# A decoder layer on one core: the input norm without GpSimd, regrouped S5 transfers, ScalarE-issued Toeplitz loads, earlier row maxima

## The chip, the cores and the metric

The kernel runs on one core of a Trainium2 chip. The metric is the device time of one execution in microseconds; three runs of the kernel before gave 2133.14, 2130.14 and 2130.84 us, median 2130.84. All inputs and outputs are float32 in HBM. Each float32 matrix product is carried out as three products of rounded parts ("high" and "low" tiles in the type fp32r: high x high, high x low, low x high), so nearly every operand has to be split on ScalarE (high copy) and VectorE (difference) before TensorE can read it.

## The reference

One layer over 1024 tokens of width 1024:

```python
h = rmsnorm(x, norm_mix)
proj = h @ w_in                      # 3 x 512 FoX, 8 log-forget, 512 S5, 4 x 512 HGRN, 3 x 1024 gates
q, k = rmsnorm(fq), rmsnorm(fk)      # per head, 8 heads x 64
y_fox = softmax(q k^T / 8 + c_i - c_j, causal) @ v      # c = cumsum(log_sigmoid(ff + bias))
y_s5 = glu(gelu(diagonal_state_space(su)))   # 32 groups x 16 channels, 64 complex states each
y_hg = rmsnorm(hgrn2(hq, hf, hi)) * silu(hg) # 4 heads, 128 x 128 state, chunks of 64
gates = sigmoid(gl)
x = x + (gates[0]*(y_fox @ wb0) + gates[1]*(y_s5 @ wb1) + gates[2]*(y_hg @ wb2)) @ w_out
x = x + cross_attention(rmsnorm(x), rmsnorm(mem))       # 4 heads, 256 memory rows
x = x + (silu(a) * b) @ w_down, where a, b = rmsnorm(x) @ w_gate_up
```

## The kernel before, in words

Activations lie with channels on the 128 partitions and tokens along the free dimension; weight tiles are the stationary operand. Every product goes through `proj`, a generator that yields after a few matmuls of 512 columns. On-chip memory is an arena of 50 equal slots (`u(name)` takes the next free one), and PSUM is handed out by bank (`psm`). A scheduler orders the instructions of each engine by a running priority; `ahead(n, fn)` emits what `fn` does as if it stood n places earlier. All DMAs before the change are issued from SP's queue, which runs them in order.

The stages run in this order: input norm and the first projections `su`, the S5 mixer, the forgetting attention (`fox_main`), the HGRN mixer (`hg_main`), then gate 0 with the branch projection of the attention, the S5 glu, gate 1, gate 2, output projection, cross attention and feed-forward. The mixers are chains of small steps on several engines, so projections of later stages are put between them as filler: `drive` runs one step of the mixer and then `pump` emits filler for a planned number of us of TensorE. In the S5 stage a step is followed by `S5_US` (4.5 us) times a weight from `S5_W`: the entries stand for preparation, its second part, the body and the output (`s5_prep`, `s5_prep2`, `s5_body`, `s5_out`, which belong to blocks o, o-1, o-2 and o-3 of a round; the round runs preparation, output, second part, body). Work given to `later(us, fn)` is emitted once the planned TensorE time has advanced by that many us.

**Input norm** (`load_x`): the eight input tiles `xk` are loaded one after another, split into `xh` (ScalarE) and `xl` (VectorE, with the norm's gain), and squared. Tiles with an even number are squared on ScalarE and added to `acc` on VectorE, the others are squared and added on GpSimd into a second sum, `accg` (tile `sq`). The row scale `Rb` comes from both sums while the first projections run.

**S5**: 32 groups are taken in eight blocks of four. `su_evac` stores the projection to the HBM tensor `su_d`; a block loads its part (`s5u`) in eight transfers, one for each of the eight time steps of a chunk. `s5_prep2` builds the block's Toeplitz matrix `toep` from a 16-row tile by eight transfers. `s5_body` computes the chunk states on VectorE and ends with the tile `kcs`; `s5_out` multiplies `toep` by the input and `kcs` by an output map into the bank `s5y`, and stores the gelu of it to `sz_d` in eight transfers. `sz_d` is read back as four `zt` tiles ahead of the glu.

**Forgetting attention**: 16 units (head pair p, query half, head). A unit runs through 4 or 8 key tiles: scores `st`, exponential `pf` (ScalarE), high copy `pt` (GpSimd), difference `pt` (VectorE), running sum `facc` (GpSimd), product with the values (`pv`). While a unit runs, `fox_pre` prepares the next one: row maxima (`mx`, `pmx`, `mn`), the step `chain`, which writes the negated maxima into `mc`, and `rows`, whose transposes (`mt`) give them to `q12a` and `q12b`. `fox_out` splits the running sum into `ah`, and `sums` (`sm`) adds it over keys on TensorE.

**Gates**: a gate whose projection ran earlier as filler is read back from `gz_d` (tile `gate`) and passes a sigmoid on ScalarE; the branch product is then multiplied by it (`mg`). `hy_d` holds the HGRN output (stored from `hoT`), read back for gate 2 as `ldy` and split into `yh` and `yl` by `load_parts`.

## Time and profile before

| | before |
|---|---|
| median of 3 runs | 2130.84 us |
| the profiled execution | 2138.17 us |
| its span | 2136.1 us |
| mean granted TensorE clock | 0.992 |
| busy: TensorE / VectorE / ScalarE / GpSimd | 97% / 71% / 38% / 28% |

The span runs from the first to the last instruction of the profiled execution; the time of an execution adds about 2 us around it. The shares are busy time over the span. A granted clock of 1.00 is 2.4 GHz; its lower level is 1.2 GHz.

### The profile page before, as it was taken

The page shows a single profiled execution, that of the slowest core. Times are in us where ns is not written, and L with a number is a line of the kernel's source. Part 1 is how long each engine was busy: PE and PEld are TensorE (multiplying, and loading weights), DVE is VectorE, ACT ScalarE, POOL GpSimd, SP SyncE. Part 2 cuts the span into 40 slices and gives each one's busy share as a digit, 9 for nine tenths or more (in the row PEclk, how much of TensorE's full clock was granted, in tenths as well). Part 3 has the DMA queues.
Part 4 walks back from the last instruction along what each step waited for, and adds up shares of the span by engine and source line. Part 5 has one row for each costly group of instructions (what it writes and reads, how often), then busy time and mean ns, then how long its engine had stood idle before and what let it go on. Part 6 is the DMA issues. An engine that isn't in the chain of part 4 may idle for free.

```text
span 2136.1 us, 26862 instructions
## 1 busy us (share of the span) xinstructions
PE 2079.2 (97%) x10044; PEld 1706.7 (80%) x10044; DVE 1521.9 (71%) x2229; ACT 814.8 (38%) x1268; POOL 608.2 (28%) x551
## 2 busy tenths in 40 slices
PE   7998999999999999999999999999999999999999
PEld 5887777776788878888778888878788888888887
DVE  8887898888854566545675567656897778775772
ACT  4113345545531123215434445444533333344441
POOL 4281204454543223221722100011032324221320
PEclk9999999999999999999999999999999999999999
DMA  4332221110213233235554523334232322248582
GB/s 163 137 104 74 51 75 32 40 50 30 70 46 124 73 109 123 74 99 196 194 192 154 201 92 106 119 117 135 74 120 98 124 99 99 103 150 282 189 281 99
DMA packets 121042, 250.94 MB, mean 117 GB/s; under 512 B 15816, under 2 KB 53704, under 8 KB 120912
## 3 DMA queue, kind: packets, MB, share of 16 engines
q1 hardware_dynamic: 120912, 249.23, 34.2%
q8 instruction: 79, 1.29, 0.3%
q14 instruction: 51, 0.42, 0.1%
HBM read 184.83 MB, written 63.18 MB: 116 GB/s over the span
## 4 chain that ended last, share of the span: by engine, by line
PE 59%; DVE 4%; DMA 1%; ACT 1%; issue 0%; SPq 0%; DVEq 0%; ACTq 0%
PE fp L228 27%; PE pj L228 26%; PE hs L228 2%; PE xo L228 1%; PE xs L228 1%; PE rs L228 1%; PE ho L228 0%; DVE t L246 0%; DVE tl L246 0%; DVE gate L246 0%; DMA gate<-gz_d 0%; DVE yl L246 0%; DMA wr<-xv 0%; DMA ldy<-hy_d 0%; PE xt L233 0%
## 5 line engine op out<-in xcount | busy, mean ns | idle before, releaser
L228 PE MATMUL pj<-xl,wh 128*128 128x512 f32 x784 | 315.5, 406 | 4.7 <-DVE xl L258 4.6
L228 PE MATMUL pj<-xh,wh 128*128 128x512 f32 x784 | 313.3, 405 | 6.7 <-ACT xh L243 5.8
L228 PE MATMUL pj<-xh,wl 128*128 128x512 f32 x784 | 311.7, 401 | 0.0
L246 DVE TENSOR_TENSOR wl<-wr,wh 128x1024 fp32r<-128x1024 f32 (+2 forms) x138 | 170.4, 1236 | 58.5 <-ACT wh L243 56.2
L228 PE MATMUL fp<-th,wc 128*128 128x512 f32 x640 | 206.9, 389 | 0.0
L228 PE MATMUL fp<-hh,wc 128*128 128x512 f32 x644 | 191.4, 389 | 0.0
L228 PEld LDWEIGHTS pj<-xh,wh 128*128 128x128 f32 x784 | 149.2, 190 | 40.0 <-ACT xh L243 6.1
L228 PEld LDWEIGHTS pj<-xl,wh 128*128 128x128 f32 x784 | 148.5, 190 | 37.4 <-DVE xl L258 7.1
L228 PEld LDWEIGHTS pj<-xh,wl 128*128 128x128 f32 x784 | 149.1, 190 | 30.8 <-issue 1.9
L228 PE MATMUL fp<-fx,wc 128*128 128x512 f32 x720 | 172.9, 389 | 0.0
L243 ACT ACTIVATE wh<-wr 128x1024 fp32r<-128x1024 f32 (+2 forms) x138 | 131.8, 957 | 76.8 <-DMA wr<-w_in 50.3
L228 PEld LDWEIGHTS fp<-fx,wc 128*128 128x128 f32 x720 | 135.2, 188 | 28.0
L228 PEld LDWEIGHTS fp<-hh,wc 128*128 128x128 f32 x644 | 120.9, 188 | 25.0
L228 PEld LDWEIGHTS fp<-th,wc 128*128 128x128 f32 x640 | 120.2, 188 | 24.9
L246 DVE TENSOR_TENSOR wc<-wr,wc 128x512 fp32r<-128x512 f32 (+1 forms) x116 | 108.5, 954 | 31.4 <-ACT wc L243 31.4
L246 POOL TENSOR_TENSOR dm<-dm 128x256 f32<-128x256 f32 (+1 forms) x96 | 79.5, 828 | 179.9 <-DMA dm<-w_dn 163.0
L246 POOL TENSOR_TENSOR acc<-acc,sq 128x512 f32<-128x512 f32 (+1 forms) x18 | 30.7, 1706 | 340.5 <-ACT sq L243 340.4
L228 PE MATMUL fp<-tl,wc 128*128 128x512 f32 x320 | 124.6, 389 | 0.7 <-DVE tl L246 0.7
L246 DVE TENSOR_TENSOR pt<-pf,pt 128x512 fp32r<-128x512 f32 (+1 forms) x96 | 94.4, 985 | 40.2 <-POOL pt L262 39.9
L246 POOL TENSOR_TENSOR fc<-fc,fs 128x512 f32<-128x512 f32 x40 | 58.0, 1449 | 216.2 <-ACT fs L243 216.2
L228 PE MATMUL fp<-hl,wc 128*128 128x512 f32 x280 | 108.9, 389 | 0.0
L262 POOL TENSOR_SCALAR pt<-pf 128x512 fp32r<-128x512 f32 (+1 forms) x96 | 67.7, 706 | 139.0 <-ACT pf L243 127.8
(427 smaller groups left out, 4862.3 us busy)
## 6 DMA issues: line engine op xcount, KB each, us to landing
wr<-w_in SPq DMA_DIRECT2D x48, 512.0 KB, 4.8
wr<-w_gu SPq DMA_DIRECT2D x44, 512.0 KB, 4.1
hr<-hb_d SPq DMA_DIRECT2D x35, 512.0 KB, 5.4
hb_d<-fc SPq DMA_DIRECT2D x44, 256.0 KB, 2.1
gz_d<-gz SPq DMA_DIRECT2D x20, 512.0 KB, 2.9
dm<-w_dn SPq DMA_DIRECT2D x20, 512.0 KB, 5.6
ws_d<-dm SPq DMA_DIRECT2D x20, 512.0 KB, 3.3
gate<-gz_d SPq DMA_DIRECT2D x20, 512.0 KB, 6.4
```

The source lines that it names most:

```text
L228: self.nc.tensor.matmul(out, lhsT, rhs, start=start, stop=stop)
L243: self.nc.scalar.activation(out=out, in_=in_, func=f, **kw)
L246: return (eng or self.nc.vector).tensor_tensor(out=out, in0=a, in1=b, op=op)
L262: (eng or self.nc.vector).tensor_scalar(out=out, in0=a, scalar1=s1, scalar2=s2, op0=op0, **kw)
```

## The change

It has six parts. (1) `load_x` squares all eight tiles on ScalarE and adds them on VectorE behind the last `xl`; `accg` and its addition are gone. (2) `su_d` and `sz_d` get a layout by S5 block, so that a block's load and its store are one transfer each; the store from `su_evac` becomes eight transfers, and each of the four `zt` loads eight. (3) The `toep` transfers are issued from ScalarE's queue instead of SP's. (4) `S5_W` gives more filler behind the body and less behind the output. (5) In the attention the high copy `pt` runs on ScalarE; `chain` is emitted 40 places ahead, and the GpSimd copy into `mc` is made when the unit's preparation begins; `sums` is queued for 6 us later instead of 2. (6) `load_parts` becomes a generator that is stepped through gate 1, one step after each of its eight blocks, instead of running whole before gate 2.

```diff
-S5_W = (1.0, 0.6, 1.0, 1.2)
+S5_W = (1.6, 0.6, 1.0, 0.6)
+SUM_AT = 6.0
+AH_MAX = 40
@@ load_x
-        def square(k, xk):
-            if k % 2 == 0:
-                self.sq_add(xk, acc, k, eng=nc.vector)
-                return
-            sq = accg if k == 1 else self.u("sq")
-            self.mul(sq, xk, xk, nc.gpsimd)
-            if k > 1:
-                self.add(accg, accg, sq, nc.gpsimd)
...
-            else:
-                square(k - 1, last)
-            last = xk
         self.w_load(2)
-        square(KB - 1, last)
-        return acc, accg
+        for k, xk in enumerate(xs):
+            self.sq_add(xk, acc, k, eng=nc.vector)
+        return acc
@@ fox_pre, build
+            mc = st["mc"] = self.sp.tile([P, 4, 16], F32, tag="mc", name="mc")
+            self.nc.gpsimd.tensor_copy(out=mc, in_=self.ohc[:, hd].unsqueeze(1).to_broadcast([P, 4, 16]))
...
-        return out + [chain, rows]
-    hi_pool = (0, 1, 2, 3)
+        return out + [lambda: self.ahead(AH_MAX, chain), rows]
@@ fox_main
-                if j % 4 in self.hi_pool:
-                    self.ts(pt[:, 0, q0:512], pr, 1.0, 0.0, ALU.mult, ALU.add, self.nc.gpsimd)
-                else:
-                    self.act(pt[:, 0, q0:512], pr, AF.Copy)
+                self.act(pt[:, 0, q0:512], pr, AF.Copy)
@@ fox_out
-            self.later(2.0, sums)
+            self.later(SUM_AT, sums)
@@ su_evac
-            self.nc.sync.dma_start(out=self.su_d[128 * i:128 * i + 128], in_=t)
+            for n in range(8):
+                self.nc.sync.dma_start(out=self.su_d[2 * i + n // 4][:, :, n % 4].rearrange("s h c -> h s c"),
+                                       in_=t[16 * n:16 * n + 16])
@@ s5_prep
-        for s in range(8):
-            nc.sync.dma_start(out=U[16 * s:16 * s + 16],
-                              in_=self.su_d[64 * o:64 * o + 64, s].rearrange("(g h) c -> h g c", g=4))
+        nc.sync.dma_start(out=ut[:, 0:512], in_=self.su_d[o].rearrange("s h g c -> (s h) (g c)"))
@@ s5_prep2
         for s in range(8):
-            nc.sync.dma_start(out=tz[16 * s:16 * s + 16, :, 16 * s:128], in_=ktv[:, :, 0:128 - 16 * s])
+            nc.scalar.dma_start(out=tz[16 * s:16 * s + 16, :, 16 * s:128], in_=ktv[:, :, 0:128 - 16 * s])
@@ s5_out
-        for t in range(8):
-            nc.sync.dma_start(out=self.sz_d[64 * o:64 * o + 64, t].rearrange("(g h) c -> h g c", g=4),
-                              in_=qv[16 * t:16 * t + 16])
+        nc.sync.dma_start(out=self.sz_d[o].rearrange("t h g c -> (t h) (g c)"), in_=q)
@@ run
-            self.nc.sync.dma_start(out=z, in_=self.sz_d[128 * i:128 * i + 128].rearrange("p t c -> p (t c)"))
+            for n in range(8):
+                self.nc.sync.dma_start(out=zv[16 * n:16 * n + 16],
+                                       in_=self.sz_d[2 * i + n // 4][:, :, n % 4].rearrange("t h c -> h t c"))
...
-        self.filler("gate1", self.gates(1, ys))
+        yh = []
+        self.filler("gate1", self.gates(1, ys, self.load_parts([self.hy_d[h] for h in range(4)], yh)))
...
-        self.filler("gate2", self.gates(2, self.load_parts([self.hy_d[h] for h in range(4)])))
+        self.filler("gate2", self.gates(2, yh))
@@ gates, load_parts
-    def gates(self, b, y):
+    def gates(self, b, y, side=None):
         for ob in range(8):
             yield from self.gate(b, ob, y)
+            if side is not None:
+                next(side, None)
...
             self.nc.sync.dma_start(out=t, in_=s)
+            yield
             h, l = self.u("yh", F32R), self.u("yl", F32R)
             self.split(t, h, l)
             out.append((h, l))
-        return out
+            yield
```

The order of instructions shows where the parts land. VectorE in the input norm, from the third `xl` on, in the kernel before:

```order
L258 SCALAR_TENSOR_TENSOR xl3_89<-xk_128,parT_74,xh3_81 128x1024
L246 TENSOR_TENSOR acc_94<-acc_94,sq_132 128x1024
L258 SCALAR_TENSOR_TENSOR xl4_90<-xk_135,parT_74,xh4_82 128x1024
L258 SCALAR_TENSOR_TENSOR xl5_91<-xk_142,parT_74,xh5_83 128x1024
L246 TENSOR_TENSOR acc_94<-acc_94,sq_146 128x1024
L258 SCALAR_TENSOR_TENSOR xl6_92<-xk_149,parT_74,xh6_84 128x1024
L258 SCALAR_TENSOR_TENSOR xl7_93<-xk_156,parT_74,xh7_85 128x1024
L246 TENSOR_TENSOR acc_94<-acc_94,sq_160 128x1024
L258 SCALAR_TENSOR_TENSOR acc_94<-sq_95,acc_94 128x1024
```

and in the changed kernel:

```order
L260 SCALAR_TENSOR_TENSOR xl3_89<-xk_125,parT_74,xh3_81 128x1024
L260 SCALAR_TENSOR_TENSOR xl4_90<-xk_129,parT_74,xh4_82 128x1024
L260 SCALAR_TENSOR_TENSOR xl5_91<-xk_133,parT_74,xh5_83 128x1024
L260 SCALAR_TENSOR_TENSOR xl6_92<-xk_137,parT_74,xh6_84 128x1024
L260 SCALAR_TENSOR_TENSOR xl7_93<-xk_141,parT_74,xh7_85 128x1024
L248 TENSOR_TENSOR acc_94<-acc_94,sq_148 128x1024
L248 TENSOR_TENSOR acc_94<-acc_94,sq_151 128x1024
L248 TENSOR_TENSOR acc_94<-acc_94,sq_154 128x1024
```

The sums that stood between the `xl` now all stand behind the last of them.

ScalarE at the start of the S5 stage (`s5x` and `s5u` here are the copies of `s5_prep2`, `wh` are high parts of weights), before:

```order
L243 ACTIVATE s5x_877<-s5g_995 128x512
L243 ACTIVATE s5u_868<-s5k_1000 16x512
L243 ACTIVATE s5x_941<-s5g_1103 128x512
L243 ACTIVATE s5u_932<-s5k_1108 16x512
L243 ACTIVATE wh_1137<-wr_1027 128x1024
```

and changed:

```order
L245 ACTIVATE s5x_898<-s5g_1069 128x512
L245 ACTIVATE s5u_896<-s5k_1074 16x512
L1159 DMA toep_851<-s5u_896 16x512
L1159 DMA toep_851<-s5u_896 16x4x112
L1159 DMA toep_851<-s5u_896 16x4x96
L1159 DMA toep_851<-s5u_896 16x4x80
L1159 DMA toep_851<-s5u_896 16x4x64
L1159 DMA toep_851<-s5u_896 16x4x48
L1159 DMA toep_851<-s5u_896 16x4x32
L1159 DMA toep_851<-s5u_896 16x4x16
L245 ACTIVATE wh_1204<-wr_1101 128x1024
L245 ACTIVATE s5x_982<-s5g_1176 128x512
```

Eight DMA issues now stand on this engine behind the copy of each block's 16-row tile, and ahead of the next weight's high part.

SP's queue ahead of the glu, from the third `zt` load on (`w_glu` are the glu's weights, `dm` and `ws_d` a weight product made for later), before:

```order
L1395 DMA zt_7950<-sz_d_72 128x1024
L1395 DMA zt_7952<-sz_d_72 128x1024
L1646 DMA gate_7989<-gz_d_73 128x1024
L351 DMA wr_7992<-w_glu 128x512
L2220 DMA dm_8006<-w_dn 128x4x128
L1646 DMA gate_8030<-gz_d_73 128x1024
L351 DMA wr_8033<-w_glu 128x512
L1608 DMA hy_d_71<-hoT_7662 128x1024
L2218 DMA ws_d_5468<-dm_8006 128x4x128
```

and changed:

```order
L1378 DMA zt_7874<-sz_d_72 16x8x128 x8
L1378 DMA zt_7883<-sz_d_72 16x8x128 x8
L1378 DMA zt_7892<-sz_d_72 16x8x128 x8
L1593 DMA hy_d_71<-hoT_7581 128x1024
L1631 DMA gate_7936<-gz_d_73 128x1024
L353 DMA wr_7939<-w_glu 128x512
L2205 DMA ws_d_5378<-dm_7857 128x4x128
L1631 DMA gate_7978<-gz_d_73 128x1024
L353 DMA wr_7981<-w_glu 128x512
```

The store of the HGRN output to `hy_d` stood behind the last two gate loads and the first two glu weights; now it stands ahead of them, and each `zt` load is eight transfers.

## Rows read from the trace of the kernel before

**Rows 1.** The profile's page, the whole span: busy time and share of each engine (PE is TensorE, PEld its weight loads, DVE VectorE, ACT ScalarE, POOL GpSimd), and the chain that ended last by engine.
```profile
PE 2079.2 (97%) x10044; PEld 1706.7 (80%) x10044; DVE 1521.9 (71%) x2229; ACT 814.8 (38%) x1268; POOL 608.2 (28%) x551
...
PE 59%; DVE 4%; DMA 1%; ACT 1%; issue 0%; SPq 0%; DVEq 0%; ACTq 0%
```

**Rows 2.** What TensorE's matmuls waited for, whole span: the waiting tile, the tile that came last and its engine; us in total, times, longest us.
```profile
PE s5y L228 <- DVE kcs L246: 10.1, 6, 3.3
PE sm L228 <- DVE ah L246: 8.0, 5, 2.3
PE mt L233 <- DVE mc L246: 7.9, 9, 1.7
...
PE pj L228 <- DVE xl L258: 4.6, 2, 3.1
PE pj L228 <- DVE yl L246: 4.1, 2, 3.9
```

**Rows 3.** Busy time by stretch: start and end in us, length, then busy us (x instructions) of each engine, TensorE's mean granted clock (1.00 is 2.4 GHz), the DMA engines' share and their GB/s.
```profile
150.00:200.00 50.00, 46.01 (x240) 37.76 (x239) 39.24 (x53) 16.40 (x20) 14.00 (x11) 0.97 0.31 91
200.00:250.00 50.00, 45.33 (x219) 37.52 (x217) 41.30 (x76) 11.59 (x22) 11.72 (x9) 0.93 0.16 38
250.00:300.00 50.00, 47.86 (x260) 38.33 (x261) 47.81 (x79) 25.57 (x35) 6.62 (x6) 1.00 0.19 49
...
500.00:550.00 50.00, 45.98 (x208) 35.62 (x206) 44.77 (x65) 26.29 (x45) 26.03 (x31) 0.97 0.09 27
```

**Rows 4.** Timeline of all engines in the input norm: start us, us, engine, line, operation, out<-in, count, and in brackets the idle time before it and what ended it.
```profile
25.48 2.88 POOL L246 TENSOR_TENSOR sq<-xk 128x1024 f32<-128x1024 f32 x1
26.54 2.91 DVE L258 SCALAR_TENSOR_TENSOR xl<-xk,parT,xh 128x1024 fp32r<-128x1024 f32 x1
...
29.37 3.42 DVE L246 TENSOR_TENSOR acc<-acc,sq 128x1024 f32<-128x1024 f32 x1
...
32.71 2.47 DVE L258 SCALAR_TENSOR_TENSOR xl<-xk,parT,xh 128x1024 fp32r<-128x1024 f32 x2
...
34.04 0.73 PE L228 MATMUL pj<-xl,wh 128*128 128x512 f32 x2 [1.52 <-DVE xl L258]
```

**Rows 5.** Timeline of TensorE in the second S5 block's output (`s5y`): the last two projection matmuls ahead of it, and the first that reads `kcs`.
```profile
165.55 0.40 PE L228 MATMUL pj<-xh,wh 128*128 128x512 f32 x1
165.78 0.40 PE L228 MATMUL pj<-xl,wh 128*128 128x512 f32 x1
168.80 0.80 PE L228 MATMUL s5y<-kcs,s5x 128*128 128x128 f32 x2 [2.62 <-DVE kcs L246]
```

**Rows 6.** Timeline of SP's queue in the S5 stage (each row a run of DMA issues).
```profile
209.90 5.05 SPq L1173 DMA_DIRECT2D toep<-s5u  x8
217.23 3.59 SPq L1228 DMA_DIRECT2D sz_d<-s5u  x8
```

**Rows 7.** VectorE's instruction groups from 325 to 600 us: count, busy us, mean ns of one, idle us before them and what ended it.
```profile
L246 DVE TENSOR_TENSOR pt<-pf,pt 128x512 fp32r<-128x512 f32 x43 | 53.9, 1256 | 24.2 <-POOL pt L262 24.0
```

**Rows 8.** GpSimd's groups, the same stretch.
```profile
L262 POOL TENSOR_SCALAR pt<-pf 128x512 fp32r<-128x512 f32 x43 | 32.0, 747 | 57.5 <-ACT pf L243 51.7 <-DVE pt L246 2.3 <-DVE ah L246 2.2
L246 POOL TENSOR_TENSOR facc<-facc,pf 128x512 f32<-128x512 f32 x21 | 30.9, 1469 | 4.6 <-ACT pf L243 4.6
```

**Rows 9.** ScalarE's groups, the same stretch: the exponentials by shape.
```profile
L243 ACT ACTIVATE pf<-st 128x512 f32<-128x512 f32 x43 | 25.4, 597 | 44.5 <-PE st L228 36.6 <-DVE pt L246 5.4 <-DVE fy L246 1.4
...
L243 ACT ACTIVATE pf<-st 128x384 f32<-128x384 f32 x15 | 7.3, 485 | 15.0 <-PE st L228 15.0
L243 ACT ACTIVATE pf<-st 128x256 f32<-128x256 f32 x14 | 5.3, 380 | 1.3 <-DVE ry L258 0.8 <-PE st L228 0.2
...
L243 ACT ACTIVATE pf<-st 128x128 f32<-128x128 f32 x14 | 3.7, 267 | 0.2
```

**Rows 10.** Timeline of SP's queue ahead of the glu.
```profile
966.24 2.28 SPq L1395 DMA_DIRECT2D zt<-sz_d  x4
968.61 0.58 SPq L1646 DMA_DIRECT2D gate<-gz_d  x1
...
995.39 0.33 SPq L1608 DMA_DIRECT2D hy_d<-hoT  x1
```

**Rows 11.** Timeline of ScalarE there.
```profile
992.87 1.05 ACT L243 ACTIVATE gate<-gate 128x1024 f32<-128x1024 f32 x1
993.82 3.89 ACT L243 ACTIVATE zh<-zt 128x1024 fp32r<-128x1024 f32 x4
```

**Rows 12.** The tile `gate` from 900 to 1010 us: its loads from issue to landing.
```profile
DMA to landing us min/median/max: 4.8/6.3/9.5
```

**Rows 13.** Timeline of VectorE there.
```profile
994.11 1.22 DVE L246 TENSOR_TENSOR hoT<-hoT,hgg 128x1024 f32<-128x1024 f32 x1
...
999.32 3.49 DVE L246 TENSOR_TENSOR zl<-zt,zh 128x1024 fp32r<-128x1024 f32 x3
```

**Rows 14.** Timeline of TensorE there: the first matmul of the glu.
```profile
998.51 0.62 PE L228 MATMUL pj<-zh,wh 128*128 128x512 f32 x2
```

**Rows 15.** Timeline of TensorE at the start of gate 2.
```profile
1071.06 0.79 PE L228 MATMUL pj<-yl,wh 128*128 128x512 f32 x1 [3.94 <-DVE yl L246]
1071.65 0.63 PE L228 MATMUL pj<-yh,wl 128*128 128x512 f32 x1
1072.08 0.63 PE L228 MATMUL pj<-yh,wh 128*128 128x512 f32 x1
```

More of the change, by code (lines that the diff above doesn't have):

```diff
@@ L479, in load_x @@
         self.xl = [self.u(f"xl{k}", F32R) for k in range(KB)]
-        acc, accg = self.u("acc"), self.u("sq")
+        acc = self.u("acc")
         _, ap, shape = self.wlist[0]
@@ L483, in load_x @@
         self.wraw[0], self.wrdy[0] = raw, (hi, lo)
-        def square(k, xk):
-            if k % 2 == 0:
-                self.sq_add(xk, acc, k, eng=nc.vector)
-                return
-            sq = accg if k == 1 else self.u("sq")
-            self.mul(sq, xk, xk, nc.gpsimd)
-            if k > 1:
-                self.add(accg, accg, sq, nc.gpsimd)
-        last = None
+        xs = []
         for k in range(KB):
             xk = self.u("xk")
+            xs.append(xk)
             cuts = [slice(0, NT)] if k else [slice(0, 512), slice(512, NT)]
@@ L719, in chain @@
                 self.nc.vector.tensor_reduce(out=mn, in_=st["pm"], axis=AX.X, op=ALU.max, negate=True)
-            mc = self.sp.tile([P, 4, 16], F32, tag="mc", name="mc")
+            mc = st["mc"]
             mh = self.sp.tile([P, 4], F32R, tag="mh", name="mh")
-            self.nc.gpsimd.tensor_copy(out=mc, in_=self.ohc[:, hd].unsqueeze(1).to_broadcast([P, 4, 16]))
             self.nc.vector.tensor_copy(out=mh, in_=mn)
@@ L725, in chain @@
             self.sub(mc[:, :, 9], mn, mh.bitcast(F32))
-            st["mc"] = mc
         def rows():
@@ L1225, in s5_out @@
         self.mul(q, q, y)
-        qv = q.rearrange("p (g c) -> p g c", g=4)
-        for t in range(8):
-            nc.sync.dma_start(out=self.sz_d[64 * o:64 * o + 64, t].rearrange("(g h) c -> h g c", g=4),
-                              in_=qv[16 * t:16 * t + 16])
+        nc.sync.dma_start(out=self.sz_d[o].rearrange("t h g c -> (t h) (g c)"), in_=q)
     def s5_main(self):
@@ L1331, in run @@
         nc = self.nc
-        self.su_d = self.dp.tile([512, 8, 128], F32, name="su_d")
+        self.su_d = self.dp.tile([8, 8, 16, 4, 128], F32, name="su_d")
         self.fy_d = self.dp.tile([4, P, NT], F32, name="fy_d")
         self.hy_d = self.dp.tile([4, P, NT], F32, name="hy_d")
-        self.sz_d = self.dp.tile([512, 8, 128], F32, name="sz_d")
+        self.sz_d = self.dp.tile([8, 8, 16, 4, 128], F32, name="sz_d")
         self.gz_d = self.dp.tile([24, P, NT], F32, name="gz_d")
@@ L1341, in run @@
         self.plan_rest()
-        xs = self.load_x()
+        acc = self.load_x()
         self.setup2()
@@ L1346, in run @@
             if k == 3:
-                acc, accg = xs
-                self.stt(acc, accg, 1.0 / 1024.0, acc, ALU.mult, ALU.add)
                 self.Rb = self.row_scale(acc)
@@ L1351, in run @@
                 self.later(8.0, lambda: self.col_scale(self.Rb, self.Rt, 8))
-        xs = acc = accg = None
+        acc = None
         self.filler("su", self.su_projs())
@@ L1394, in run @@
             z = self.u("zt")
-            self.nc.sync.dma_start(out=z, in_=self.sz_d[128 * i:128 * i + 128].rearrange("p t c -> p (t c)"))
+            zv = z.rearrange("p (t c) -> p t c", t=8)
+            for n in range(8):
+                self.nc.sync.dma_start(out=zv[16 * n:16 * n + 16],
+                                       in_=self.sz_d[2 * i + n // 4][:, :, n % 4].rearrange("t h c -> h t c"))
             zt.append(z)
@@ L1679, in glu, with load_parts @@
             yield from self.proj(f"glu{i}", lambda k: zs[k], ev(i), nk=4)
-    def load_parts(self, srcs):
-        out = []
+    def load_parts(self, srcs, out):
         for s in srcs:
```

## The prediction, made before the changed kernel was run

> **What bounds the kernel now.** I began with the engine shares: TensorE is busy 2079.2 of the 2136.1 us span and holds 59% of the chain that ended last; VectorE holds 4%, DMA and ScalarE 1% each [rows 1]. So work taken off VectorE, ScalarE or GpSimd gives nothing by itself. Only the 57 us in which TensorE stands idle can be won, and the stretches in which its clock is granted at the lower level. The table of TensorE's waits [rows 2] says which tile was late each time: `kcs` (S5 states) 10.1 us, `ah` (row sums) 8.0, `mc` (negated row maxima) 7.9, `xl` (input's low part) 4.6, `yl` (HGRN output's low part) 4.1. All five come from VectorE, and the change touches the surroundings of each. The table by stretches [rows 3] shows the second cost: where a long stall ends, the mean granted clock of the 50 us falls below 1.00 (0.97, 0.93 and 0.97; 1.00 in the fourth row). TensorE stood idle for 2 to 3 us ahead of each, and runs behind it at 1.2 instead of 2.4 GHz for a few us. (1 − 0.97) x 50 = 1.5 us and (1 − 0.93) x 50 = 3.5 us bound what each costs.
>
> **Input norm.** Before, GpSimd squares and adds four of the eight input tiles. While it does, one VectorE `xl` takes 2.91 us and one `acc` add 3.42; two `xl` after it, 2.47 together, so 1.24 each [rows 4]. The second of those released TensorE at 34.04 after 1.52 us, the last of the `xl` stalls. The change squares all eight on ScalarE and puts seven adds (1.2 us each by the same 1.24, 8.4 in all) behind the last `xl`, as the order of VectorE shows. The `xl` then keep 1.24 and come before each block of 12 matmuls that reads them (12 x 0.23 = 2.8 us, the step from 165.55 to 165.78 in [rows 5]), so the whole 4.6 us should go. The added sum is hidden as long as it is ready when the block's norm wants it, after the last `xl` block. If that cover were gone, 8.4 us against the four slow adds removed would cost some 2 us. I take −4.6, bounds −5 to −2.
>
> **S5 stage.** Per block of four groups, SP spends 5.05 us issuing eight `toep` transfers and 3.59 issuing eight `sz_d` stores [rows 6], and about as much for eight `s5u` loads. The change makes the stores and loads one each, and moves the `toep` issues to ScalarE, in order between its `wh` copies. But SP is nowhere named as what TensorE waited for; `kcs` is, from a VectorE that is 39 to 41 of 50 us busy [rows 3]. What can help is the new weight list: filler after the body goes from 1.0 to 1.6, so the planner puts more projection matmuls between the body's start and `kcs`. Before, TensorE ran out at 165.78 and stood 2.62 us [rows 5]. 0.6 more of a unit (`S5_US`, 4.5 us) is 2.7 us of matmuls, just the size of that stall; the longest, 3.3 [rows 2], would be left with 0.6. But the order shows that the added matmuls aren't spread evenly. Of six stalls with 10.1 us I leave two, 3 us together, with one short clock stretch (1.5): 10.1 + 1.5 + 3.5 − 4.5 = 10.6, so −11. Bounds: all of it, −15; or, where ScalarE's eight issues delay a `wh`, and with it VectorE's `wl`, −3. No row has a DMA issued from ScalarE; SP's 0.63 each (5.05 / 8) is the nearest, so 64 issues are 40 us of ScalarE in 200 us in which it is about a third busy.
>
> **Forgetting attention.** Every `pt` high copy leaves GpSimd for ScalarE. VectorE's subtraction behind it has a mean of 1.26 us and waited 24.0 us for GpSimd in this stretch [rows 7]; GpSimd's own copy takes 0.75 and its sum 1.47 [rows 8]. A copy on ScalarE is bounded by the exponentials of the same shapes, 0.27 to 0.60 us [rows 9]; in their mix (41.7 us for 86) 96 copies cost 46 us over some 300. ScalarE goes from 26 [rows 3] to some 34 of 50 us, still below full. With earlier `pt`, VectorE has room. The three other edits act straight on the stalls: the row sums are queued 6 instead of 2 us after the attention output, so `ah` (two VectorE subtractions that end up to 2.3 us late [rows 2]) should be ready every time; the row-maximum chain is given a priority ahead of its neighbours, and its GpSimd copy sits in the unit's start instead of the chain. Of `ah` 8.0 and `mc` 7.9 I take 7.5 and 6, and the clock stretch of 500 to 550 us (1.5): −15. Bounds: −19, nearly all; −6, when ScalarE's longer queue delays `q12a` and the exponentials and TensorE waits for these instead.
>
> By the Trainium skill, "SBUF — State Buffer", section "SBUF: two separate sides", GpSimd and a VectorE instruction with two SBUF inputs exclude each other for a whole instruction; the 2.91 against 1.24 us of [rows 4] agrees. By that rule the `facc` sums, which stay on GpSimd, would go on blocking the subtractions, and the fox term would be worth less (an estimate: on 512 columns the sums take 30.9 us and the copies 32.0 [rows 8], so half, −7); by the rows, which give a stall's price, it is −15.
>
> **Branch projections and glu.** Here I see a loss. Before, SP issues four `zt` loads at 966.24 within 2.28 us, then the gates of blocks 6 and 7 (the first at 968.61), and only then the store `hy_d`, which waits until 995.39 for the HGRN output [rows 10]. In the changed order 32 `zt` loads stand there (at 2.28 / 4 = 0.57 each 18 us, by 984, still ahead of 995), then `hy_d`, and *behind it* both gates and two glu weights. Nothing on SP passes a waiting instruction. So gate 6 is issued at about 995, lands 6.3 us later (4.8 to 9.5 [rows 12]), at 1001; gate 7 with it or 1 us after. ScalarE's sigmoids (1.05 each) stand ahead of the `zh` copies in its order: before, gate 992.87, then four `zh` from 993.82 in 3.89 us [rows 11]. After: gates 1001 to 1003, first `zh` at 1004, last `zl` at 1008 (before, 999.32 + 3.49 = 1002.8 [rows 13]). TensorE reads the first `zh` at 998.51 without wait [rows 14], so it would stand 5 to 6 us. Then 1.5 to 3.5 us of lower clock, as after the other stalls. +8; bounds 0 (the store is ready earlier because stages before gain, and the gates land in time) and +13 (landing 9.5).
>
> **HGRN loads.** The four `ldy` loads and splits move from one block after gate 1 into its course. Before, TensorE stood 3.94 us on `yl` until 1071.06, then ran with matmuls 0.43 us apart instead of 0.23 [rows 15], losing about half of some 5 us. Spread over gate 1, eight blocks of at least 24 matmuls (24 x 0.23 = 5.5 us each), the splits have some 40 us. −4.1 − 2.6 = −6.7, bounds −3 and −7.5.
>
> **Sum.** −4.6 − 11 − 15 + 8 − 6.7 = −29.3 against the profiled execution, 2138.2 us (span 2136.1), gives 2108.9. The profiled one is 7.3 us above the runs' median of 2130.84, so 2101.6: 2102 us, 1.4% less. (A change below 0.2%, 4.3 us, can't be told from none.)
>
> **Rivals.**
> *The gates aren't late*: the HGRN norm runs earlier, so `hy_d` doesn't hold SP. For it: the store only waits for one VectorE pair; against: `hoT` ends at 995 and the first glu matmul is at 998.5, 3.5 us for a 6.3 us landing. Without the +8: 2094.
> *ScalarE becomes the queue that stalls*: 40 us of issues and 46 us of copies sit between `wh`, `pf` and `q12a`. For it: all of these stand in one queue in order; against: it is half idle [rows 3]. If each S5 block loses 1.4 us more, and half of fox's gain goes, 11 + 7.5 back: 2120.
> *The S5 part doesn't do what it says*: VectorE is as loaded as before there, and filler put in one place is missing in another, since the weights sum to 3.8 before and after. Stalls only move, −11 drops out: 2113.
> *Slower than before*: a DMA issue on ScalarE costs much more than SP's 0.63. S5's eight blocks last 200 us; over 150 of them ScalarE is busy 16.4 + 11.6 + 25.6 = 54 us [rows 3], so it has 16 free in a block's 25, which eight issues fill at 2.0 us each. Beyond, every 0.1 us costs 6.4 us over 64. To lose 29.3 + 4.3 = 34 us it must cost 2.0 + 0.53 = 2.5 us each. At 2.7: 2101.6 + 45 = 2146. Nothing in the rows of either queue comes near.
>
> By the Trainium skill, "DMA: Bandwidth & Descriptors", section "Issuing engines are not separate DMA queues", issuing from another engine saves only the sequencer's time. By that rule the move itself is worth nothing, since SP isn't waited for; [rows 2] agree, and my −11 is put on the filler weights alone.
>
> **How the numbers follow.** My forecast 0.50, gates not late 0.17, ScalarE stalls 0.15, S5 unchanged 0.12, slower 0.06 (half of it within 0.2%). The unknown bounds of the five terms, taken as independent, are about ±12 us around 2102 (2090 to 2114); the range reaches to the ScalarE rival above and the late-gate rival below: 2086 to 2122. Faster 0.92, same 0.04, slower 0.04.
>
> **What would show it.** Right: no `xl`, `sm` or `yl` row over 1 us in TensorE's waits; `kcs` under 4; a new wait on `zh` or `zl` of 4 to 7 us near the glu with a granted clock below 1.00 behind it; ScalarE some 50 us busier. Wrong: `kcs` again near 10; waits for `wh`, `q12a` or `pf` in their place; gaps of more than 1 us on ScalarE around each `toep` issue; no stall at glu.

## The result: slower

The changed kernel took 2160.86 us (median of 4 runs, 2154.97 to 2163.65), the kernel before in the same job 2131.99. The ratio is 1.0132, 95% interval 1.0107 to 1.0156: about 28 us slower, where 29 us faster was forecast (2102 us, range 2086 to 2122). The profiled execution took 2159.73 us, its span is 2157.8 (2136.1 before), its mean granted clock 0.986 (0.992 before).

The page after, the lines that answer to [rows 1]:

```profile
PE 2085.0 (97%) x10044; PEld 1713.0 (79%) x10044; DVE 1498.3 (69%) x2232; ACT 862.1 (40%) x1366; POOL 534.7 (25%) x448
...
PE 67%; DVE 7%; ACT 3%; DMA 2%; issue 1%; POOL 1%; SPq 0%; DVEq 0%; ACTq 0%
```

TensorE is still busy 97% of a longer span, with 6 us more in its busy time, which is slower clock, not work: the instruction count is the same. VectorE's share of the chain that ended last rose from 4% to 7%, ScalarE's from 1% to 3%. What TensorE waited for, which answers to [rows 2]:

```profile
PE s5y L230 <- DVE kcs L248: 16.6, 4, 6.1
PE pj L230 <- DVE wl L248: 10.2, 8, 3.7
...
PE mt L235 <- DVE mc L248: 5.7, 5, 2.8
...
PE pv L230 <- DVE pt L248: 3.6, 5, 2.1
PE mx L230 <- DVE pmx L705: 3.2, 1, 3.2
PE hst L230 <- ACT hbT L245: 3.0, 1, 3.0
...
PE pj L230 <- ACT zh L245: 2.5, 1, 2.5
...
PE sm L230 <- DVE ah L248: 1.6, 1, 1.6
```

Here the forecast went wrong in a way that one can read. `xl` and `yl` are gone, `ah` fell from 8.0 to 1.6 us, `mc` from 7.9 to 5.7. But `kcs` rose from 10.1 to 16.6, `wl` from 1.9 to 10.2, and new ones came, the largest for `pt` 3.6, `pmx` 3.2, `hbT` 3.0 and `zh` 2.5. The stretches after (compare [rows 3]):

```profile
50.00:100.00 50.00, 44.95 (x189) 36.05 (x188) 37.96 (x143) 6.38 (x6) 10.47 (x30) 0.97 0.47 144
...
300.00:350.00 50.00, 38.61 (x185) 31.45 (x184) 44.19 (x83) 21.12 (x33) 3.29 (x5) 0.90 0.20 69
...
1000.00:1050.00 50.00, 44.55 (x176) 34.92 (x176) 31.11 (x37) 25.71 (x36) 10.41 (x8) 0.93 0.58 195
```

From 50 to 100 us TensorE now stands idle 5 us, from 300 to 350 it stands 11.4 us and has the lower clock for a fifth of the time (0.90), and from 1000 to 1050 5.4 us.

To place the loss by stage I summed, from the starts of TensorE's matmuls in each trace, the time by which a step from one matmul to the next exceeds the usual step of its kind in the kernel before (this counts stalls and lower clock alike). The difference of the totals, 22.5 us, is near that of the spans, 21.7:

| us lost | input norm | to the end of S5 | attention | HGRN | gate 0 and glu | gates 1, 2 | rest | total |
|---|---|---|---|---|---|---|---|---|
| before | 10.7 | 27.7 | 43.4 | 34.0 | 2.0 | 8.0 | 26.8 | 152.5 |
| after | 4.0 | 44.3 | 47.8 | 40.3 | 10.9 | 2.0 | 25.5 | 175.0 |
| `su_d` as before | 5.7 | 36.0 | 47.8 | 38.4 | 10.9 | 2.1 | 24.9 | 165.8 |
| `sz_d` as before | 4.2 | 42.5 | 49.4 | 38.3 | 2.4 | 2.0 | 27.3 | 166.2 |
| before + input norm | 2.7 | 26.1 | 44.9 | 33.5 | 2.0 | 7.9 | 27.2 | 144.3 |
| before + S5 weights | 11.4 | 39.4 | 49.6 | 32.0 | 2.0 | 8.5 | 26.3 | 169.1 |
| before + `toep` on ScalarE | 10.4 | 37.9 | 47.1 | 29.4 | 2.0 | 6.7 | 25.3 | 158.8 |
| before + high copies | 12.4 | 27.2 | 37.9 | 31.1 | 2.0 | 6.9 | 25.5 | 142.9 |
| before + row sums | 11.4 | 26.0 | 48.8 | 38.5 | 2.4 | 6.1 | 26.8 | 160.1 |

One profile can be off by 2 to 3 us in a stage (the first column of the rows with the old norm runs from 10.4 to 12.4), so the verdicts below go by the timed ratios.

### The profile page after: what moved, and what is told of

Same layout as the page of the kernel before. It is cut to its first block, busy times and chain, and to the rows that moved or that the text cites. A ratio compares the mean times of both kernels' runs of the same rounds, so it can differ in the third digit from the quotient of the medians.

```text
span 2157.8 us, 26872 instructions
## 1 busy us (share of the span) xinstructions
PE 2085.0 (97%) x10044; PEld 1713.0 (79%) x10044; DVE 1498.3 (69%) x2232; ACT 862.1 (40%) x1366; POOL 534.7 (25%) x448
## 4 chain that ended last, share of the span: by engine, by line
PE 67%; DVE 7%; ACT 3%; DMA 2%; issue 1%; POOL 1%; SPq 0%; DVEq 0%; ACTq 0%
PE pj L230 30%; PE fp L230 27%; PE hs L230 2%; PE st L230 1%; PE xo L230 1%; PE rs L230 1%; PE xs L230 1%; PE pv L230 1%; PE ho L230 1%; DVE wl L248 0%; PE mx L230 0%; DVE t L248 0%; ACT wh L245 0%; DVE ry L260 0%; DMA gate<-gz_d 0%
## 5 line engine op out<-in xcount | busy, mean ns | idle before, releaser
L230 PEld LDWEIGHTS pj<-xh,wh 128*128 128x128 f32 x784 | 149.6, 191 | 42.5 <-ACT xh L245 6.6
L248 POOL TENSOR_TENSOR dm<-dm 128x256 f32<-128x256 f32 (+1 forms) x96 | 88.4, 921 | 159.5 <-DMA dm<-w_dn 125.5
L248 POOL TENSOR_TENSOR facc<-facc,pf 128x256 f32<-128x256 f32 (+1 forms) x64 | 70.7, 1105 | 122.7 <-ACT pf L245 116.9
L248 DVE TENSOR_TENSOR pt<-pf,pt 128x512 fp32r<-128x512 f32 (+1 forms) x96 | 72.8, 761 | 38.4 <-ACT pt L245 37.9
```

The costliest lines, as they stand in the source:

```text
L230: self.nc.tensor.matmul(out, lhsT, rhs, start=start, stop=stop)
L248: return (eng or self.nc.vector).tensor_tensor(out=out, in0=a, in1=b, op=op)
```

## The experiments

"The changed kernel" is the one of the result, "before" the one ahead of it; every ratio is against before, in the same job, with its 95% interval.

### The regrouped transfers

```diff
# a_su_old: the changed kernel, hunks of su_d reversed
-            for n in range(8):
-                self.nc.sync.dma_start(out=self.su_d[2 * i + n // 4][:, :, n % 4]...
+            self.nc.sync.dma_start(out=self.su_d[128 * i:128 * i + 128], in_=t)
# a_sz_old: the changed kernel, hunks of sz_d reversed
-            for n in range(8):
-                self.nc.sync.dma_start(out=zv[16 * n:16 * n + 16], ...
+            self.nc.sync.dma_start(out=z, in_=self.sz_d[128 * i:128 * i + 128]...
```

> The changed kernel with su_d in its old layout: four stores of 512 KB instead of 32 of 64 KB, and eight loads for each S5 block again. Theory (SP's queue): the 32 stores take 0.47 us each of SP's issuing between 41 and 75 us, the weight loads behind them come late, and TensorE waits 5.5 us for weights' high and low parts between 56 and 74 us, with 1.7 us of lower clock behind. So these waits vanish and the time falls by 6 to 8 us. Rival (the VectorE sums of the new input norm push the weights' low parts back): the waits between 56 and 74 us stay and the time moves by less than 2 us.

Measured: 1.0084 (1.0064 to 1.0104), 10 us below the changed kernel, somewhat more than expected. SP's queue in the changed kernel, from 40 us on:

```profile
41.46 7.49 SPq L876 DMA_DIRECT2D su_d<-su  x16
...
50.94 6.88 SPq L876 DMA_DIRECT2D su_d<-su  x8
```

TensorE there (the bracket is the idle time before, and what ended it):

```profile
73.56 0.50 PE L230 MATMUL pj<-xh,wl 128*128 128x512 f32 x1 [3.73 <-DVE wl L248]
```

24 of the 32 stores hold SP 14.4 us, the weights behind them come late, and VectorE, which takes its instructions in order, splits the next weight only behind a run of small S5 steps that had stood waiting with it. The waits between 50 and 76 us are gone with four stores. The trace has 0.45 to 0.86 us for the issue of 64 KB, and 0.33 to 1.07 for one of 512 KB in the kernel before: the number counts, not the size. The Trainium skill, "DMA: Bandwidth & Descriptors", section "Rules for kernel authors", wants small transfers joined into large ones, and this run agrees (10 us); the change joined them at one end of `su_d` and split them at the other.

> The changed kernel with sz_d in its old layout: four zt loads instead of 32, eight stores for each S5 block again. Theory (the hy_d store stands on SP ahead of the last gate loads because the 32 zt loads pushed those back): the gates go ahead of the store again, TensorE's waits from 1012 to 1026 us (2.4 + 2.6 + 1.0) and the two stretches of lower clock there (3.4 us each, 1.7 lost in each) vanish: 8 to 10 us less. Rival (the gates are late because of the order alone, not through the zt loads): waits stay, under 2 us of change; eight stores more for each S5 block could also cost some us in the S5 stage.

Measured: 1.0090 (1.0067 to 1.0114), 9 us below the changed kernel (the intervals just overlap); the waits for `zh` and the lower clock at 1016 and 1026 us are gone. The changed kernel's SP queue ahead of the glu (compare [rows 10]):

```profile
986.54 18.34 SPq L1378 DMA_DIRECT2D zt<-sz_d  x32
1014.92 0.34 SPq L1593 DMA_DIRECT2D hy_d<-hoT  x1
1015.35 0.38 SPq L1631 DMA_DIRECT2D gate<-gz_d  x1
```

and ScalarE and TensorE there (compare [rows 11] and [rows 14]):

```profile
1020.03 1.06 ACT L245 ACTIVATE gate<-gate 128x1024 f32<-128x1024 f32 x1 [8.05 <-DMA gate<-gz_d]
...
1024.84 0.73 PE L230 MATMUL pj<-zh,wh 128*128 128x512 f32 x2 [2.46 <-ACT zh L245]
```

This is the forecast's loss, as told: 32 `zt` issues in 18.3 us (18 forecast), the `hy_d` store waits until 1014.92, both gates stand behind it, and ScalarE stands 8.05 us for the first of them with the `zh` copies behind. TensorE's waits come out smaller than the 5 to 6 us forecast, 2.5 for `zh` and 0.8 for `zl`; 2.2 us for a weight's `wl` just ahead (gone too with four loads) and two stretches of lower clock make up the rest.

### The `toep` transfers on ScalarE

```diff
# b_tp: the kernel before; b_tp_half takes nc.scalar for odd s only; a_tp_sp: the changed kernel, reversed
-            nc.sync.dma_start(out=tz[16 * s:16 * s + 16, :, 16 * s:128], ...
+            nc.scalar.dma_start(out=tz[16 * s:16 * s + 16, :, 16 * s:128], ...
```

> The kernel before with the toep transfers on ScalarE's queue alone. Theory (SP's issues weren't waited for, and ScalarE has room): within 3 us of before. Rival (ScalarE's issues hold back the weights' high parts and the S5 copies; this is the part of the S5 stage's loss that su_d and the weights leave): kcs and wl waits rise and the time by 6 to 10 us.

> The kernel before with every second toep transfer on ScalarE's queue, the others on SP's. Theory (the cost comes from the issuing on ScalarE, so it goes with its number): half of 9 us, 3 to 6 us above before; ScalarE held 2.5 to 4 us at a time. Rival (the cost comes from the order into which the scheduler puts the filler, 30 projection matmuls instead of 59 under the first body): either all of it, 8 to 11 us, or, where the order stays, nothing.

> The changed kernel with the toep transfers back on SP's queue. Theory (on ScalarE's queue the eight issues of a block hold its computing for 5 to 8 us and the scheduler puts less filler under the first bodies; this is what su_d leaves of the S5 stage's loss): waits for kcs and for ScalarE's tiles fall, 7 to 10 us less, as the toep move alone cost 9 us. Rival (the cost belongs to the move only in the old arrangement, and the single loads, stores and new weights carry the S5 loss here): less than 4 us won.

Measured: all eight 1.0044 (1.0029 to 1.0059), 9 us slower; half of them 1.0016 (1.0005 to 1.0026), 3 us. ScalarE with all eight (a row with ACTq is a run of issues):

```profile
115.59 6.28 ACTq L1170 DMA_DIRECT2D toep<-s5u  x8
121.91 1.06 ACT L245 ACTIVATE wh<-wr 128x1024 fp32r<-128x1024 f32 x1 [6.35 <-DMA toep<-s5u]
...
158.49 8.02 ACTq L1170 DMA_DIRECT2D toep<-s5u  x8
166.56 1.06 ACT L245 ACTIVATE wh<-wr 128x1024 fp32r<-128x1024 f32 x1 [8.10 <-DMA toep<-s5u]
```

Of the eight blocks six issue all eight in one piece, in 5.2 to 8.0 us (0.65 to 1.0 each), and the next instruction waits 4.3 to 8.1 us. For the same eight in one piece SP had taken 5.05 to 5.8 us in the kernel before: the issue itself costs about as much on either queue, but on ScalarE computing stands behind it. TensorE's waits from 100 to 330 us, first with all eight, then with half:

```profile
PE s5y L230 <- DVE kcs L248: 12.8, 6, 6.1
PE rs L230 <- ACT sq L245: 2.4, 2, 1.7
PE pj L230 <- DVE wl L248: 1.9, 1, 1.9
PE s5d L230 <- ACT s5x L245: 1.2, 1, 1.2
```

```profile
PE s5y L230 <- DVE kcs L248: 12.8, 6, 6.1
PE pj L230 <- DVE wl L248: 0.7, 1, 0.7
PE rs L230 <- ACT sq L245: 0.6, 1, 0.6
```

`kcs` is 12.8 in both (10.1 before), so the scheduler's other placing of the filler doesn't make the difference between the two; ScalarE's tiles and the `wl` that hang on them do: 2.4 + 1.9 + 1.2 with eight, 0.6 + 0.7 with four. Half the issues cost 3 us, as expected of a cost that goes with their number. The named waits fall by more than half (5.5 to 1.3 us), as if a hold of 2.6 to 4.1 us fitted between ScalarE's tasks better than one of 5 to 8; the times, 3 and 9 us with 2 to 3 us of interval on each side, don't show that. In the changed kernel the reversal gave only 1.0115 (1.0096 to 1.0135), some 4 us and not clear of no gain, as the rival said. What holds the S5 stage up there instead is not shown; `kcs` is still 14.0 us.

### The S5 filler weights

```diff
# b_w: the kernel before; a_w_old: the changed kernel, reversed
-S5_W = (1.0, 0.6, 1.0, 1.2)
+S5_W = (1.6, 0.6, 1.0, 0.6)
# c_npl_w2: c_norm_pt_ldy (below) with
+S5_W = (0.7, 0.6, 1.0, 1.5)
# c_noxfer: the changed kernel, with the hunks of su_d, sz_d and toep reversed
```

> The changed kernel with the old filler weights of the S5 stage. Theory (the new weights place the body of a block so that GpSimd's preparation of the next one lies over its VectorE chain, and the last blocks run out of filler): TensorE's wait for kcs goes from 16.6 back to about 10 us and the lower clock in the S5 stage from 17 to about 10 us of stretch, together 8 to 12 us less. Rival (the ScalarE-issued toep transfers or the single loads do it): kcs stays above 14 us, the time moves by less than 4 us.

> The changed kernel without its three transfer edits (su_d, sz_d and toep as before): input norm, filler weights, attention edits and HGRN loads. Theory (the transfers carry the whole loss, and the four others are worth the input norm's 9 us and little more): 7 to 12 us below before, with the weights within 3 us of nothing. Rival (the parts work against each other in the arena and in the scheduler's order, HGRN loss of 6 us and attention loss of 4 us stay without the transfers): within 3 us of before.

> The kernel before with the new filler weights of the S5 stage alone. Theory (the weights, not the transfers, put the body of a block under the next block's preparation and take filler from the second body: with old transfers and the input norm the S5 stage lost 14 us): kcs waits rise to 13 to 17 us and the lower clock in the S5 stage to over 20 us of stretch, 8 to 15 us above before. Rival (as forecast, more filler behind the body covers kcs): kcs under 4 us, 8 to 13 us below before.

> Input norm, high copies on ScalarE and HGRN loads, with the S5 filler weights moved the other way: 0.7 behind the body and 1.5 behind the output (1.0 and 1.2 before, 1.6 and 0.6 in the change). Theory (more filler in one place starts the next block's chain late and is missing elsewhere, so a shift either way costs): the S5 stage loses 4 to 15 us more than with the old weights. Rival (kcs stalls come from too much filler ahead of the body's chain, and less of it helps): kcs under 8 us, 3 to 8 us below the same kernel with the old weights.

Measured: in the changed kernel the old weights give only 1.0113 (1.0097 to 1.0129), no clear gain, and without the transfer edits the rest is still at 1.0058 (1.0038 to 1.0078): both misses of mine, which sent me to the weights alone. They cost 16 us by themselves, 1.0074 (1.0059 to 1.0089), about as expected; shifted the other way they cost 28 (1.0075 against 0.9940 with the old ones), where 15 at most was expected. TensorE's longest wait of the whole span with the new weights (before, `kcs` with 10.1), then with the opposite ones:

```profile
PE s5y L230 <- DVE kcs L248: 13.9, 5, 4.2
```

```profile
PE rs L230 <- ACT sq L245: 18.4, 4, 9.8
```

More filler behind the body didn't cover `kcs`; it rose. Less of it brought `kcs` down to 5.0 us, and the time rose more. So it isn't a question of more cover for `kcs`. Stretches of the kernel before, then with the new weights (VectorE is the third busy time):

```profile
100.00:300.00 200.00, 189.20 (x984) 154.89 (x983) 171.98 (x266) 59.70 (x86) 69.49 (x49) 0.97 0.26 74
300.00:350.00 50.00, 47.47 (x237) 37.79 (x235) 43.83 (x86) 28.38 (x46) 10.35 (x17) 1.00 0.24 74
```

```profile
100.00:300.00 200.00, 189.57 (x978) 155.46 (x977) 151.03 (x238) 58.83 (x85) 64.41 (x48) 0.97 0.24 72
300.00:350.00 50.00, 36.75 (x164) 30.33 (x163) 45.23 (x84) 19.49 (x28) 3.94 (x6) 0.83 0.27 76
```

VectorE did 172.0 us of work from 100 to 300, with the new weights 151.0 (154.2 with the opposite ones). The 21 us that are missing come due at the stage's end, where TensorE is busy 36.75 of 50 us at a clock of 0.83: between 100 and 352 us it ran 27 us at the lower level, 10 before. What VectorE waited for from 100 to 300, before and with the new weights:

```profile
DVE gz L246 <- PE pj L228: 4.7, 3, 2.4
```

```profile
DVE gz L248 <- PE pj L230: 17.3, 7, 4.7
DVE wl L248 <- ACT wh L245: 11.8, 3, 8.1
```

`gz` is the reading of a finished filler product: in VectorE's order it stands ahead of S5 steps, so filler put in one place makes VectorE wait for TensorE there, and TensorE for VectorE later. This is read from these waits; no run moves the `gz` readings alone. The wait for `wl` beside it hangs on ScalarE's `wh` and is not followed here. For the opposite shift the account doesn't hold: its trace has no `gz` row among VectorE's waits from 100 to 300 us, and what TensorE waited for is `sq`, squares for the norm of the attention's queries and keys, made on ScalarE. ScalarE was late with them for more than one reason (a weight that had not landed, then VectorE's `qs`), so why that shift costs 28 us stays open.

### The attention's edits

```diff
# b_pt: the kernel before, high copies alone (a_pt_pool: the changed kernel, reversed)
-                    self.ts(pt[:, 0, q0:512], pr, 1.0, 0.0, ALU.mult, ALU.add, self.nc.gpsimd)
+                self.act(pt[:, 0, q0:512], pr, AF.Copy)
# b_sm: the kernel before, row sums alone
-            self.later(2.0, sums)
+            self.later(6.0, sums)
# b_fox: the kernel before with both, and with mc early and chain 40 places ahead
# c_norm_smmc: the kernel before with the input norm and all of b_fox but the high copies
```

> The changed kernel with the attention's high copies back on GpSimd. Theory (ScalarE's longer queue gave back in new waits what the other attention edits won: 4.7 us for pt, 3.2 for pmx, 2.7 for q12a and q12b): these fall to about 2 us and the time by 4 to 8 us. Rival (the copy is what freed VectorE, and without it ah and mc are late again): ah and mc waits go from 7 to 12 us or more, the time rises by 4 to 8 us.

> The kernel before with the attention's edits alone (high copies on ScalarE, row sums at 6 us, row-maximum chain 40 places ahead with its copy early). Theory (the forecast's mechanism with its new waits: ah and mc waits fall from 16 to 7 us, and waits for pt, pmx and q12a take about as much back; the filler left over lies otherwise in the HGRN stage, where a 3.0 us wait for hbT appears): the time is 0 to 8 us above before, with an hbT wait in the trace. Rival (the attention edits do win by themselves, and the changed kernel's attention and HGRN losses come from the S5 stage ahead of it): 6 to 15 us below before, no hbT wait.

> The kernel before with the input norm and two of the attention's edits (row sums at 6 us, row-maximum chain ahead), the high copies left on GpSimd. Theory (VectorE's load in the attention sets the stalls, and moving the sums and the chain only moves them: ah and mc waits fall by 10 us, others take most of it back): within 4 us of the input norm alone, so 5 to 12 us below before. Rival (the copies on ScalarE are what took the gain back): ah and mc waits fall and nothing comes for them, 14 to 22 us below before.

> The kernel before with the attention's high copies on ScalarE alone. Theory (the copies free VectorE of GpSimd's port and are worth something, and the sums and the chain took it back): waits for ah and mc fall from 16 to 8 to 12 us, no hbT wait, 4 to 8 us below before. Rival (the copies only pass TensorE's wait from GpSimd's tiles on to ScalarE's): within 3 us of before.

> The kernel before with the attention's row sums at 6 us instead of 2 alone. Theory (the row sums' late place alone takes the ah wait away, at most 2 us of it stay, and the hbT wait in the HGRN stage comes from the other part, the chain 40 places ahead): 5 to 9 us below before, no hbT wait. Rival (the sums' place shifts the filler, and what is left meets the HGRN steps otherwise): hbT wait of 3 us, new waits for pt and pmx, within 3 us of before or above.

Measured: all together nothing, 1.0006 (0.9996 to 1.0016). The copies alone win 8 us, 0.9963 (0.9948 to 0.9978), at the upper end of what I expected, and some 6 are lost when they are taken out of the changed kernel (1.0161, 1.0143 to 1.0179; the intervals overlap). The later row sums alone lose 8, 1.0040 (1.0025 to 1.0055), where I had expected 5 to 9 gained; sums and chain put on top of the input norm cost its whole gain (1.0013, 0.9999 to 1.0027), which neither theory nor rival had. The chain was never run alone; by difference it costs between nothing and 4 us. TensorE's waits from 325 to 620 us, with the copies alone, then with the later sums alone:

```profile
PE mt L235 <- DVE mc L248: 7.0, 7, 1.6
PE sm L230 <- DVE ah L248: 2.7, 5, 1.1
```

```profile
PE mt L235 <- DVE mc L248: 6.4, 7, 2.4
PE pv L230 <- DVE pt L248: 3.9, 6, 1.4
PE mx L230 <- DVE pmx L714: 3.2, 1, 3.2
...
PE sm L230 <- DVE ah L248: 0.9, 1, 0.9
```

Later sums do clear `ah`, as forecast, and `pt`, `pmx` and, in the HGRN stage, `hbT` (3.0 us) take its place. VectorE at the `pmx` stall with the later sums:

```profile
439.59 1.65 DVE L248 TENSOR_TENSOR pt<-pf,pt 128x512 fp32r<-128x512 f32 x1
...
442.18 1.76 DVE L248 TENSOR_TENSOR pt<-pf,pt 128x512 fp32r<-128x512 f32 x1
443.87 1.62 DVE L260 SCALAR_TENSOR_TENSOR qs<-qs,gq,ry 128x1024 f32<-128x1024 f32 x1
445.42 0.68 DVE L714 TENSOR_REDUCE pmx<-mx 128x1 f32<-128x512 f32 x1
```

It has no gap: two differences of 1.7 us beside GpSimd, a scaling of 1.6, and only then the maximum that frees the bank for TensorE. With the copies on ScalarE the difference itself gets shorter (VectorE's group from 325 to 600 us, compare [rows 7]):

```profile
L248 DVE TENSOR_TENSOR pt<-pf,pt 128x512 fp32r<-128x512 f32 x43 | 42.7, 998 | 21.6 <-ACT pt L245 21.0
```

1.26 to 1.00 us, 11 us of VectorE in this row alone, while its wait for the high copy (24.0 to 21.0) hardly changes. That the 8 us come from this freed time, and not from the other order of ScalarE and GpSimd, is argued from the two rows; no run separates them.

### Input norm, HGRN loads, and the best combination

```diff
# b_norm: the kernel before with the change's load_x; c_norm_pt: and with b_pt's line
# b_ldy: the kernel before with the change's gates and load_parts; c_norm_pt_ldy: all three
+        for k, xk in enumerate(xs):
+            self.sq_add(xk, acc, k, eng=nc.vector)
...
+            if side is not None:
+                next(side, None)
```

> The kernel before with the input norm of the change alone. Theory (the xl stalls go and the sums behind them are hidden): TensorE's xl waits, 4.6 us, vanish, nothing else moves: 4 to 7 us less. Rival (the arena's slots rotate otherwise, and stages that follow meet new waits, as the S5 stage of the changed kernel with 8 us more that neither su_d nor the weights explain): the S5 stage loses 5 to 8 us in turn, and the time is within 3 us of before.

> The kernel before with the HGRN loads stepped through gate 1 alone. Theory: TensorE's yl wait of 4.1 us and the lower clock behind it vanish, nothing else moves: 5 to 7 us less. Rival (VectorE and ScalarE work moved into gate 1 delays its gates): less than 3 us won.

> The kernel before with input norm, high copies on ScalarE and HGRN loads through gate 1: the parts that the runs so far let win or be neutral. Theory: the norm's 8 us and 4 to 8 us of the copies add up, 10 to 16 us below before. Rival (the scheduler's order doesn't let parts add up, as with weights and toep, which together cost less than each alone): no better than the norm alone, 5 to 10 us below before.

> The kernel before with the input norm and the high copies on ScalarE, the HGRN loads as before. Theory (the HGRN loads gained nothing alone: yl's wait went over to weights behind a held SP queue): as fast as with the HGRN loads, 12 to 15 us below before. Rival (they are worth 4 us here, where the stages ahead are shorter): 8 to 11 us below before.

Measured: the norm 0.9954 (0.9940 to 0.9969), the HGRN loads 0.9995 (0.9984 to 1.0007), norm and copies 0.9947 (0.9934 to 0.9961), all three 0.9940 (0.9923 to 0.9957). The last is the fastest kernel of the study, 2122.19 us against 2135.37; the HGRN loads' part in it can't be told from none. TensorE's waits from 990 to 1130 us with the HGRN loads alone:

```profile
PE pj L230 <- DVE wl L248: 2.6, 2, 2.5
PE pj L230 <- ACT wh L245: 1.9, 2, 0.9
```

`yl` is gone, but 4.5 us of weights came for it. The longest two, 0.94 us at 1074.13 and 2.46 at 1077.33, hang on ScalarE's order:

```profile
1072.51 1.06 ACT L245 ACTIVATE mh<-mg 128x1024 fp32r<-128x1024 f32 x1 [7.79 <-DVE mg L248]
1073.47 0.61 ACT L245 ACTIVATE wh<-wr 128x512 fp32r<-128x512 f32 x1
```

The next weight's high part stands behind `mh`, the high copy of a finished gate product, and VectorE ended that product (`mg`) only at 1072.4: it had worked through the 12 us before with one gap of 0.35 us, a `yl` of 2.85 us among its work. So without the `yl` wait TensorE arrives earlier at a chain that isn't ready earlier. A held SP queue, which I had taken for the cause, is not what is new: the store `ws_d` waits for GpSimd's product, with gate and weight loads behind it, 16 us there and 22 us in the kernel before, which has no wait for weights. First with the HGRN loads alone, then before:

```profile
1057.19 0.51 SPq L2220 DMA_DIRECT2D dm<-w_dn  x1
1073.84 0.38 SPq L2218 DMA_DIRECT2D ws_d<-dm  x1
```

```profile
1053.59 0.61 SPq L2220 DMA_DIRECT2D dm<-w_dn  x1
1076.50 0.38 SPq L2218 DMA_DIRECT2D ws_d<-dm  x1
```

## Why the prediction was wrong

**What bounds the kernel.** "So work taken off VectorE, ScalarE or GpSimd gives nothing by itself", read from shares of the whole span, did not hold: with the copies gone from GpSimd, VectorE is busy 11 us less in the attention (231 to 220 from 325 to 600 us), and the time fell by 8.

**Input norm (−4.6).** Right in mechanism and too small: 10 us by the ratio. The loss summed over the stage fell by 8 us where the named waits held 4.6.

**S5 (−11).** Wrong in sign, in three steps. "What can help is the new weight list": alone it costs 16 us; I had counted the filler that covers one stall and not what VectorE does while that filler runs (its 39 to 41 of 50 us busy left out the third row of [rows 3], 47.81). "SP is nowhere named as what TensorE waited for", taken as a price of nothing for the regrouping: I listed loads and stores of the S5 blocks, but not the 32 stores of `su_evac`, which the diff shows and which stand on SP ahead of weights (10 us). And the `toep` issues: 0.63 us each was near (0.65 to 1.0), ScalarE "about a third busy" was true, but a share over 50 us says nothing about an in-order queue that is held for 8 us in one piece (9 us alone; priced at most 8 in the bound, and more in the rival). The rival for slower asked for 2.5 us an issue and did not come; the time was lost in the other ways named here.

**Attention (−15).** Wrong: 0. The waits named were taken as separate prices, but all came from a VectorE that is busy 231 of 275 us there; the later row sums, an edit of order, moved the wait to the next tile on VectorE. The edit that takes work time off VectorE, the copies, won 8, and it was the one to which I had put no price of its own. The Trainium skill's rule on the shared port ("SBUF — State Buffer", section "SBUF: two separate sides"), which I had set aside for the rows, points at that edit; 1.26 to 1.00 us agrees with it. That the copies' 8 us are near the 7 which the forecast had worked out with it is luck: the 7 were half the price of all stalls of the stage, and the stage as a whole won nothing.

**Glu (+8).** Right in place, cause and size: 9 us, with shorter waits on `zh` and `zl` (3.3 us instead of 5 to 6) and more beside them.

**HGRN loads (−6.7).** The stall went as told, but nothing was won alone: I took TensorE's next weights to be ready, and they hang on `mg` and `mh`, which the loads don't hasten. In the changed kernel the gates 1 and 2 did lose 6 us less; no run takes the loads back out there, so it isn't shown that they bring it.

**HGRN stage (0).** Unpriced: 6 us in the changed kernel, of which the later row sums bring 4.5 by themselves, with the `hbT` wait.

The effects, −10 norm, +16 weights, −8 copies, +8.5 sums, +9 `toep`, −1 loads alone on the kernel before, and +10 `su_d`, +9 `sz_d` by reversal in the changed one, add to +34 us; 28 were measured. That weights and `toep` partly cover each other fits both reversals (a_w_old, a_tp_sp: 4 us each, where they cost 16 and 9 alone). Of the rivals, "ScalarE becomes the queue that stalls" held for one part; none had a planner's weight that costs, and my chance of 0.04 for slower rested on adding every part's gain as if sure.

## What to carry to other kernels

Where TensorE's waits name several tiles of one engine, price that engine's time and not the waits: here the later sums, an edit of order, moved them, and the two edits that shortened VectorE's instructions (norm, copies) won. Count every DMA issue on every queue at both ends of a changed layout, and look at what stands behind each; a mean share doesn't show a hold in one piece. Try the parts of a bundle one by one: here two of nine effects won, and those two alone run 0.5% below the kernel before, 1.8% below the changed one.

## What was not expected of the hardware

A DMA issue on ScalarE took 0.65 to 1.0 us (5.2 to 8.0 us for eight), on SP 0.63 to 0.73 (5.05 to 5.8); the computing that stood behind it on ScalarE waited that long. The lower clock adds to the stalls: the changed kernel has 14 stretches with 62 us at 1.2 GHz, the kernel before 8 with 38. Half of the 24 us more, 12 at most and less where TensorE stood idle in them, is clock, of the 21.7 us by which the two profiled executions differ. It also falls without a stall: in the kernel before, from 750 to 800 us, TensorE is busy all 50 us at a granted clock of 0.90; the first fall there, at 769 us, comes behind a run of 16 small matmuls (`hs`).
